# Another order of the seven block products of a feed-forward unit, and four extra buffers where its input sums are made

## The chip, the core and the metric

The kernel runs on one core of a Trainium2 chip. The metric is the device time of one execution in microseconds (us). The engines named below are PE (TensorE: matmuls, in its own order), ACT (ScalarE), DVE (VectorE), POOL (GpSimd) and SP, which issues the DMAs. Each takes its instructions in the order in which the program gives them to it.

## What is computed

The reference is a two-layer trunk over 512 latent and 256 context tokens of width 1024. Each layer has a gated feed-forward half (D_FF 2816), a mixer (a convolution in layer 0, neighbourhood attention in layer 1) and a second feed-forward half. The part that matters here:

```python
def _rmsnorm(x, g): return (x * rsqrt(mean(x * x) + 1e-6)) * g
def _ffn_half(s, mod, g, wg, wu, wd):
    shift, scale, gate = mod
    h = _rmsnorm(s, g) * (1 + scale) + shift
    return s + 0.5 * gate * ((silu(h @ wg) * (h @ wu)) @ wd)
def layer(i):
    x, xc = ffn_half(x, ...), ffn_half(xc, ...)      # first half
    x, xc = x + gate * mixer(x), xc + gate * mixer(xc)
    x, xc = ffn_half(x, ...), ffn_half(xc, ...)      # second half
```

Four feed-forward halves follow each other with the mixers between them. The change concerns the two in the middle (called ffn1 and ffn2 below: the second half of layer 0 and the first of layer 1), which run back to back.

## The kernel before

Activations lie with the 1024 channels on partitions (8 tiles `x0` to `x7` of 512 latent columns, 8 tiles `xc0` to `xc7` of 256 context columns). A matmul is made of three in a reduced fp32 format: an operand v is split into `hi` (a rounded copy, written by ACT) and `lo` (v minus hi, written by DVE), and hi*hi, hi*lo and lo*hi are added up in PSUM. `split` (L114 to L116) writes both parts.

In ffn1 and ffn2 the matrix product is done by a Strassen-like scheme with seven block products in place of eight. Channels and tokens are halved: columns are two blocks of 386 (384 tokens and two columns of shift). `s_prepare` (L445) makes, for each pair j of channel tiles (j = 0 to 3), the scaled activations `sx` and their sums and differences `tt`, and splits all of it: product 1 takes one block ("ones"), products 2 and 3 share a pair of tiles, so do 5 and 6, and 7 and 4. These tiles are slots of two rings: `h` (16 slots in pool main, which also hold `z`, the input of the product `pw2` at the end of the convolution, L806 to L828) and `hx` (12 slots). `s_prepare` runs in that loop after every second `pw2` product, and again in the last `down` loop of ffn1, for ffn2.

`s_weights` (L375) loads one weight unit, makes four sums in `s12` and `s34` on DVE (L398 to L402), and splits into four tiles, which this text calls A (products 1 and 2, from `raw`), B (6 and 5, from `s12`), C (7 and 3, from `s34`) and D (4, from `raw`, half as wide). `whi` and `wlo` are rings of three buffers, so A of the next unit takes the buffers of B, B those of C, C those of D, and D those of its own unit's A: each can be written once PE has finished the products of the tile before it in the buffer.

`s_unit` (L407) runs the seven products, 12 matmuls of 386 columns each, in three PSUM banks: x (`a`) holds 1, then 6 on top, 7 on top, 4 on top; y (`b`) holds 2; z (`c`) holds 5, then 3 on top. Between them partial sums leave the banks: `kept` (ACT, L422) copies one aside before the next product is added, and DVE adds rows (L429, L435, L437). A unit of the gate matrix (then a multiplication by `rb` on DVE, L487, and Silu on ACT, L489) and a unit of the up matrix make a pair; `s_ffn` (L475) runs groups of 2, 2, 2, 2 and 3 pairs, each followed by its `down` products (L125 to L127, L510). That is 11 pairs or 22 units in each of ffn1 and ffn2.

The order on each engine is not written by hand. The program is built with a scheduler that simulates the engines and emits whatever is ready by its own clock, so a changed order of the source moves instructions on all of them.

Of the kernel before, what the change touches and what calls it, by code (L numbers as in the profile page):

```python
# [23 lines left out]
T = TL + TC  # L24
# [3 lines left out]
BLK = 384  # L28
# [30 lines left out]
def tile_trunk(ctx: ExitStack, tc, xin, cb, cs, par, modp, modv, gu, gs, dn, pw1, pw2, wqk, wv, wo, bv, rpb, out):  # L59
# [38 lines left out]
    def X(c, s):  # L98
        return xc[c] if s else xl[c]
# [264 lines left out]
    def blocks(ap):  # L364
        return ap.rearrange("p (b n) -> p b n", b=2)
# [10 lines left out]
    def s_weights(src, pool):  # L376

        raws = []
        for i in range(2):
            raw = main.tile([P, 1024], F32, tag="raw", name="raw", bufs=4)  # L380
            nc.sync.dma_start(raw, src[i])
            raws.append(raw)
        q = [raws[0][:, :512], raws[0][:, 512:], raws[1][:, 512:], raws[1][:, :512]]
        s12 = pool.tile([P, 1024], F32, tag="s12", name="s12", bufs=1)
        s34 = pool.tile([P, 1024], F32, tag="s34", name="s34", bufs=1)
        s1, s2, s3, s4 = s12[:, 512:], s12[:, :512], s34[:, :512], s34[:, 512:]
        made = {}

        def parts_of(t, names):
            n = 512 * len(names)  # L390
            hi = main.tile([P, 1024], F32R, tag="whi", name="whi", bufs=3)
            lo = main.tile([P, 1024], F32R, tag="wlo", name="wlo", bufs=3)
            split(hi[:, :n], lo[:, :n], t[:, :n])
            for i, name in enumerate(names):
                made[name] = (hi, lo, 512 * i)

        parts_of(raws[0], (1, 2))
        nc.vector.tensor_tensor(s1, q[2], q[3], ALU.add)  # L398
        nc.vector.tensor_tensor(s2, s1, q[0], ALU.subtract)
        parts_of(s12, (6, 5))  # L400
        nc.vector.tensor_tensor(s3, q[0], q[2], ALU.subtract)
        nc.vector.tensor_tensor(s4, q[1], s2, ALU.subtract)  # L402
        parts_of(s34, (7, 3))
        parts_of(raws[1], (4,))
        return made

    def s_unit(src, hs, pool, row):  # L407

        made = s_weights(src, pool)

        def product(name, p, first):
# [24 lines left out]
        product(3, z, False)
        nc.vector.tensor_tensor(row[:, 0, 1], z, b, ALU.add)  # L437
        product(4, x, False)
        nc.scalar.activation(row[:, 1, 0], x, AF.Copy)

    def s_row(pool, tag):
        return pool.tile([P, 2, 2, SB], F32, tag=tag, name=tag, bufs=1)

    def s_prepare(j, hs, pool, A, B):

        sx = s_row(pool, "sg")
        tt = s_row(pool, "tu").rearrange("p a b n -> p (a b) n")
        for r in range(2):
            c = 2 * j + r
            for s in range(2):  # L450
                o, e, _ = PARTS2[s]
                nc.scalar.activation(sx[:, r, :, o:e], blocks(X(c, s)), AF.Identity, scale=A[:, s, c:c + 1])
            nc.gpsimd.tensor_copy(sx[:, r, :, BLK:], B[:, :, c].rearrange("p (a b) -> p a b", a=1).broadcast_to([P, 2, 2]))
        of = pool if j < 2 else None
        if j % 2 == 0:
            hs[1] = hs.get(1, []) + [None, None]
            ones_ = [slot() for _ in range(2)]
            for i in range(2):
                hs[1][j + i] = tuple(t[:, i * SB:(i + 1) * SB] for t in ones_)
        split(*hs[1][j], sx[:, 0, 0])  # L460

        def two(names, src):
            to = [slot(of) for _ in range(2)]
            split(*(t.rearrange("p (a n) -> p a n", a=2) for t in to), src)
            for i, n in enumerate(names):
                hs.setdefault(n, []).append(tuple(t[:, i * SB:(i + 1) * SB] for t in to))

        two((2, 3), sx[:, 1])
        nc.vector.tensor_tensor(tt[:, 0], sx[:, 0, 1], sx[:, 0, 0], ALU.subtract)
        nc.vector.tensor_tensor(tt[:, 1], sx[:, 1, 1], tt[:, 0], ALU.subtract)  # L470
        two((5, 6), tt[:, :2])
        nc.vector.tensor_tensor(tt[:, 2], sx[:, 1, 1], sx[:, 0, 1], ALU.subtract)
        nc.vector.tensor_tensor(tt[:, 3], sx[:, 1, 0], tt[:, 1], ALU.subtract)
        two((7, 4), tt[:, 2:])

    def s_ffn(idx, hs, hid, gate, done=None, tail=None):
        pair = 0
        for gi, gn in enumerate(PAIRS):
            last = gi == len(PAIRS) - 1
            hids = []  # L480
            f0 = 2 * pair
            for i in range(gn):
                sg, tu = s_row(hid, "sg"), s_row(hid, "tu")
                s_unit(gs[idx - 1, pair, 0], hs, hid, sg)
                for r in range(2):
                    so = sg[:, r, :, :BLK]
                    nc.vector.tensor_tensor(so, so, rbk, ALU.mult)  # L487
                    for o, e, s in PARTS2:
                        nc.scalar.activation(so[:, :, o:e], so[:, :, o:e], AF.Silu, bias=sg[:, r, 0, BLK + s:BLK + s + 1])  # L489
                s_unit(gs[idx - 1, pair, 1], hs, hid, tu)  # L490
                for r in range(2):
                    to = tu[:, r, :, :BLK]
                    if i < 2:
                        h2 = [hid.tile([P, T], F32R, tag="hid", name="hid", bufs=8) for _ in range(2)]
                    else:
                        h2 = [slot(hid if tail else None)[:, :T] for _ in range(2)]
                    h2 = [blocks(t) for t in h2]
                    nc.vector.tensor_tensor(to, to, rbk, ALU.mult)
                    for o, e, s in PARTS2:
                        nc.vector.scalar_tensor_tensor(to[:, :, o:e], to[:, :, o:e], tu[:, r, 0, BLK + s:BLK + s + 1],  # L500
                                                       sg[:, r, :, o:e], ALU.add, ALU.mult)
                    split(*h2, to)
                    hids.append(h2)
                pair += 1

            def down_one(d, w, st):
                o, e, s = PARTS2[st is CTX]
                p = pc(TC) if s else ps()
                mm3(blocks(p), w, [tuple(t[:, :, o:e] for t in h2) for h2 in hids], None, None)
                nc.vector.scalar_tensor_tensor(XS(d, st), p, derv[gate][:, s, d:d + 1], XS(d, st), ALU.mult, ALU.add)  # L510
                if last:
                    square_in(d, st)

            for sts in ((LAT,), (CTX,)) if last and tail else (BOTH,):
                for d in range(NC):
                    w = load(dn[idx, d, :, f0 * P:(f0 + 2 * gn) * P], 2 * gn * P)
                    for st in sts:
                        down_one(d, w, st)
# [286 lines left out]
    with tc.tile_pool(name="ffn12", bufs=1) as hid:  # L805
        hs = {}  # L806
        for d in range(NC):
# [16 lines left out]
            for st in BOTH:  # L824
                square_in(d, st)
            if d % 2:
                s_prepare(d // 2, hs, hid, derv[0, 7], mods[0, 6])
        s_rows(BOTH)  # L828

        hs2 = {}  # L830
# [301 lines left out]
```

## Time and profile before

| what | value |
|---|---|
| median of 3 runs | 2699.73 us (2698.58 to 2699.76) |
| the profiled execution, its own time | 2700.21 us |
| its span (first to last instruction in the trace) | 2698.4 us |
| PE busy | 2629.3 us, 97% of the span |
| DVE busy | 1905.2 us, 71% |
| ACT busy | 985.1 us, 37% |
| ffn1 and ffn2 with the end of the convolution | about 830 to 1990 us of the span |

A busy share says how long instructions of an engine were under way, not that it could not have been faster. What a wait costs is read from the idle time ahead of an instruction, in square brackets behind it in a timeline, with what ended it.

### The profile page before, as it was taken

The numbers are of one execution on the slowest core, as the hardware profiler recorded it, in microseconds if no ns is written. First come the engines' busy times: TensorE is split into PE (matmuls) and PEld (weight loads), VectorE is DVE, ScalarE is ACT, GpSimd is POOL, SyncE is SP. The second block draws the span as 40 slices with busy tenths as digits, with TensorE's granted clock in tenths as the row PEclk, the third lists the DMA queues.
The fourth block names the chain that finished last, engine by engine and source line by source line (L and its number), as shares of the span: only waits on it lengthen the run. The fifth ranks groups of instructions, "written<-read, shape, count | busy, mean of one in ns | idle before, by whom it ended". The sixth has DMA issues, their size and how long they took to land.

```text
span 2698.4 us, 40901 instructions
## 1 busy us (share of the span) xinstructions
PE 2629.3 (97%) x16420; PEld 2358.1 (87%) x16420; DVE 1905.2 (71%) x3268; ACT 985.1 (37%) x1601; POOL 77.5 (3%) x140
## 2 busy tenths in 40 slices
PE   8999999999989899999999999999999999999997
PEld 4888888888859799999999999999888888999997
DVE  4999999857996766666777666667677576544446
ACT  4212121232226533433454234334446365322224
POOL 0000000011020100000001000000000000000001
PEclk9999999999999899999999999999999999999999
DMA  8565656622351122122121221221332211233223
GB/s 303 167 205 171 207 174 229 235 73 84 97 119 48 36 75 67 55 78 67 61 80 40 82 67 51 71 80 59 116 101 62 64 61 48 72 103 100 87 96 108
DMA packets 97262, 276.66 MB, mean 103 GB/s; under 512 B 11568, under 2 KB 26032, under 8 KB 96944
## 3 DMA queue, kind: packets, MB, share of 16 engines
q1 hardware_dynamic: 96496, 272.48, 31.7%
q8 instruction: 129, 2.11, 0.3%
q0 software_dynamic: 576, 1.57, 0.2%
q14 instruction: 61, 0.50, 0.1%
HBM read 268.05 MB, written 4.38 MB: 101 GB/s over the span
## 4 chain that ended last, share of the span: by engine, by line
PE 90%; DVE 4%; issue 2%; ACT 2%; DMA 1%; POOL 1%; SPq 0%; DVEq 0%; POOLq 0%; ACTq 0%
PE a L417 13%; PE a L125 8%; PE a L127 8%; PE a L126 8%; PE c L417 6%; PE c L125 6%; PE c L126 6%; PE c L127 6%; PE b L125 5%; PE b L126 5%; PE b L127 5%; PE b L417 3%; PE st L975 2%; PE b L966 1%; DVE y L691 1%
## 5 line engine op out<-in xcount | busy, mean ns | idle before, releaser
L110 ACT ACTIVATE whi<-raw 128x1024 fp32r<-128x1024 f32 (+3 forms) x304 | 270.0, 891 | 862.2 <-PE c L126 454.3
L111 DVE TENSOR_TENSOR wlo<-raw,whi 128x1024 fp32r<-128x1024 f32 (+3 forms) x304 | 306.0, 1009 | 89.8 <-ACT whi L110 87.7
L549 DVE SCALAR_TENSOR_TENSOR junk<-mraw,sbc 128x1024 f32<-128x1024 f32 x224 | 272.8, 1218 | 1.7
L125 PE MATMUL a<-h,whi 128*128 128x512 f32 (+2 forms) x826 | 270.0, 328 | 1.1 <-DVE sg L301 1.1
L127 PE MATMUL a<-h,wlo 128*128 128x512 f32 (+2 forms) x826 | 269.0, 326 | 0.9 <-DVE wlo L111 0.9
L126 PE MATMUL a<-h,whi 128*128 128x512 f32 (+2 forms) x826 | 269.0, 326 | 0.0
L417 PE MATMUL a<-h,whi 128*128 128x386 f32 x880 | 234.8, 345 | 21.9 <-ACT whi L115 19.5
L125 PE MATMUL c<-h,whi 128*128 128x258 f32 (+2 forms) x768 | 233.1, 306 | 1.2 <-ACT h L115 1.1
L126 PE MATMUL c<-h,whi 128*128 128x258 f32 (+2 forms) x768 | 233.3, 305 | 0.6 <-DVE h L116 0.6
L127 PE MATMUL c<-h,wlo 128*128 128x258 f32 (+2 forms) x768 | 232.4, 303 | 0.0
L417 PEld LDWEIGHTS a<-h,whi 128*128 128x128 f32 x880 | 160.0, 190 | 30.9 <-ACT whi L115 26.2
L125 PE MATMUL b<-h,whi 128*128 128x512 f32 (+2 forms) x550 | 181.7, 330 | 5.3 <-ACT h L237 3.4
L126 PE MATMUL b<-h,whi 128*128 128x512 f32 (+2 forms) x550 | 180.8, 329 | 0.5 <-DVE h L238 0.5
L127 PE MATMUL b<-h,wlo 128*128 128x512 f32 (+2 forms) x550 | 180.4, 328 | 0.0
L115 ACT ACTIVATE whi<-s 128x1024 fp32r<-128x1024 f32 x88 | 93.5, 1062 | 229.1 <-PE c L417 126.7
L125 PEld LDWEIGHTS a<-h,whi 128*128 128x128 f32 x826 | 155.8, 189 | 16.9 <-DVE sg L301 2.0
L127 PEld LDWEIGHTS a<-h,wlo 128*128 128x128 f32 x826 | 156.1, 189 | 15.6 <-DVE wlo L111 1.6
L126 PEld LDWEIGHTS a<-h,whi 128*128 128x128 f32 x826 | 156.2, 189 | 14.1 <-issue 0.8
L126 PEld LDWEIGHTS c<-h,whi 128*128 128x128 f32 x768 | 145.3, 189 | 8.6 <-DVE h L116 1.2
L125 PEld LDWEIGHTS c<-h,whi 128*128 128x128 f32 x768 | 144.1, 188 | 9.6 <-ACT h L115 1.5
L127 PEld LDWEIGHTS c<-h,wlo 128*128 128x128 f32 x768 | 145.7, 190 | 6.6 <-issue 0.6
L417 PE MATMUL a<-h,wlo 128*128 128x386 f32 x440 | 149.4, 340 | 0.0
(305 smaller groups left out, 6388.7 us busy)
## 6 DMA issues: line engine op xcount, KB each, us to landing
mraw<-in_modv SPq DMA_DIRECT2D x128, 512.0 KB
raw<-in_gu SPq DMA_DIRECT2D x88, 512.0 KB
raw<-in_gs SPq DMA_DIRECT2D x88, 512.0 KB
raw<-in_dn SPq DMA_DIRECT2D x64, 384.0 KB
raw<-in_dn SPq DMA_DIRECT2D x64, 256.0 KB
raw<-in_pw SPq DMA_DIRECT2D x24, 512.0 KB
raw<-in_dn SPq DMA_DIRECT2D x32, 320.0 KB
us<-v SPq DMA_DIRECT2D x64, 142.0 KB
```

The source lines that it names most:

```text
L110: nc.scalar.activation(hi[:, :cols], raw[:, :cols], AF.Copy)
L111: nc.vector.tensor_tensor(lo[:, :cols], raw[:, :cols], hi[:, :cols].bitcast(F32), ALU.subtract)
L115: nc.scalar.activation(hi, src, AF.Copy)
L125: nc.tensor.matmul(po, lhsT=whi[:, s], rhs=ah, start=first and i == 0, stop=False)
L126: nc.tensor.matmul(po, lhsT=whi[:, s], rhs=al, start=False, stop=False)
L127: nc.tensor.matmul(po, lhsT=wlo[:, s], rhs=ah, start=False, stop=last and i == k - 1)
L417: nc.tensor.matmul(p, lhsT=a[:, k], rhs=b, start=first and j == 0 and i == 0, stop=j == 3 and i == 2, skip_group_check=True)
L549: nc.vector.scalar_tensor_tensor(junk, raw, 1.0, sbc[:, s, :], ALU.mult, ALU.mult, accum_out=m[:, s, c:c + 1])
L691: nc.vector.scalar_tensor_tensor(yo, u[:, k:k + n], w, yo, ALU.mult, ALU.add)
L966: nc.tensor.transpose(pt[:, i * P:(i + 1) * P], p[:, i * P:(i + 1) * P], ident)
L975: nc.tensor.matmul(po[64 * a:64 * a + 64, :P], lhsT=v[:, c0:c0 + 64], rhs=PT[a][:, i * P:(i + 1) * P], start=i == 0, stop=i == 3)
```

## The change

In `s_unit` the order of the products is 1, 2, 5, 6, 3, 7, 4 in place of 1, 2, 6, 5, 7, 3, 4. In `s_prepare` the call at the end of the convolution (`early=True`) takes `sx` and `tt` from the ring `hid` (8 buffers, so two j are under way at once; `hid` tiles become 772 wide in place of 768) and no longer from the single `sg` and `tu`. The slots are dealt out otherwise: "ones" of all j, (2, 3) of j 0 and 1, and (5, 6) and (7, 4) of j 0 come from `hx`, all others from `h`; before, all of j 0 and 1 but "ones" came from `hx`, and "ones" and all of j 2 and 3 from `h`. In `s_weights` two DVE subtractions change places.

```diff
@@ s_weights
+        nc.vector.tensor_tensor(s4, q[1], s2, ALU.subtract)
         nc.vector.tensor_tensor(s3, q[0], q[2], ALU.subtract)
-        nc.vector.tensor_tensor(s4, q[1], s2, ALU.subtract)
@@ s_unit
+        product(5, z, True)
+        d = kept(z)
         product(6, x, False)
         b = kept(x)
-        product(5, z, True)
-        d = kept(z)
+        product(3, z, False)
+        nc.vector.tensor_tensor(row[:, 0, 1], z, b, ALU.add)
         product(7, x, False)
         nc.vector.tensor_tensor(row[:, 1, 1], x, d, ALU.add)
-        product(3, z, False)
-        nc.vector.tensor_tensor(row[:, 0, 1], z, b, ALU.add)
         product(4, x, False)
@@ s_prepare
-    def s_prepare(j, hs, pool, A, B):
-        sx = s_row(pool, "sg")
-        tt = s_row(pool, "tu").rearrange("p a b n -> p (a b) n")
+    def s_prepare(j, hs, pool, A, B, early=False):
+        if early:
+            sx = [pool.tile([P, TB], F32, tag="hid", name="sx", bufs=8) for _ in range(2)]
+            tt = [pool.tile([P, TB], F32, tag="hid", name="tt", bufs=8) for _ in range(2)]
...
-        of = pool if j < 2 else None
-            ones_ = [slot() for _ in range(2)]
+            ones_ = [slot(pool) for _ in range(2)]
...
-        two((2, 3), sx[:, 1])
+        two((2, 3), sx[1], pool if j < 2 else None)
...
-        two((5, 6), tt[:, :2])
+        two((5, 6), tt[0], pool if j < 1 else None)
...
-        two((7, 4), tt[:, 2:])
+        two((7, 4), tt[1], pool if j < 1 else None)
@@ end of the convolution
-                s_prepare(d // 2, hs, hid, derv[0, 7], mods[0, 6])
+                s_prepare(d // 2, hs, hid, derv[0, 7], mods[0, 6], True)
```

First place: PE in the second group of ffn1, where a gate unit passes into its up unit. Before (bank `a_9394` is x of the gate unit, `c_9396` its z, `a_9523` and `b_9524` are x and y of the up unit, `whi_9503` is the up unit's A, `whi_9386` the gate unit's C):

```order
L417 MATMUL a_9394<-h_8518,whi_9380 128x386
L417 MATMUL a_9394<-h_8519,whi_9380 128x386
L417 MATMUL a_9394<-h_8518,wlo_9381 128x386
L417 MATMUL c_9396<-h_8518,wlo_9381 128x386
L417 MATMUL a_9523<-h_7840,whi_9503 128x386
L417 MATMUL a_9523<-h_7841,whi_9503 128x386
L417 MATMUL b_9524<-hx_7844,whi_9503 128x386
L417 MATMUL b_9524<-hx_7845,whi_9503 128x386
L417 MATMUL a_9394<-hx_7856,whi_9386 128x386
```

The same place in the changed program (`a_9402` and `c_9404` are x and z of the gate unit, `whi_9394` its C, `whi_9511` the up unit's A):

```order
L417 MATMUL a_9402<-h_8526,whi_9388 128x386
L417 MATMUL a_9402<-h_8527,whi_9388 128x386
L417 MATMUL a_9402<-h_8526,wlo_9389 128x386
L417 MATMUL c_9404<-hx_7846,whi_9394 128x386
...
L417 MATMUL c_9404<-h_8520,wlo_9395 128x386
L417 MATMUL a_9531<-hx_7842,whi_9511 128x386
L417 MATMUL a_9531<-hx_7843,whi_9511 128x386
L417 MATMUL b_9532<-hx_7846,whi_9511 128x386
L417 MATMUL b_9532<-hx_7847,whi_9511 128x386
L417 MATMUL a_9402<-hx_7858,whi_9394 128x386
```

The first four matmuls of the up unit, which need its A, stood right behind products 6 and 5; now the 12 matmuls of product 3 stand between.

Second place: ACT and DVE where the up unit of that pair passes into the gate unit of the next. ACT before, from the up unit's C (`whi_9515`) to the next gate unit's A (`whi_9642`); L439 and L489 still belong to the gate unit of the first pair:

```order
L115 ACTIVATE whi_9515<-s34_9502 128x1024
L439 ACTIVATE sg_9366<-a_9394 128x386
L115 ACTIVATE whi_9519<-raw_9499 128x512
L489 ACTIVATE sg_9366<-sg_9366 128x2x256
L489 ACTIVATE sg_9366<-sg_9366 128x2x128
L422 ACTIVATE kept_9565<-a_9523 128x386
L115 ACTIVATE whi_9642<-raw_9636 128x1024
```

ACT in the changed program (Silu is L494 there), from the up unit's C (`whi_9523`) to the next gate unit's A (`whi_9650`):

```order
L115 ACTIVATE whi_9523<-s34_9510 128x1024
L115 ACTIVATE whi_9527<-raw_9507 128x512
L439 ACTIVATE sg_9374<-a_9402 128x386
L422 ACTIVATE kept_9573<-c_9533 128x386
L494 ACTIVATE sg_9374<-sg_9374 128x2x256
L494 ACTIVATE sg_9374<-sg_9374 128x2x128
L115 ACTIVATE whi_9650<-raw_9644 128x1024
```

The two Silu instructions now stand right ahead of the next unit's A. DVE at the same place, before (L487 is the multiplication that the Silu waits for):

```order
L116 TENSOR_TENSOR wlo_9516<-s34_9502,whi_9515 128x1024
L487 TENSOR_TENSOR sg_9366<-sg_9366,rb_81 128x2x384
L429 TENSOR_TENSOR tu_9367<-b_9524,kept_9538 128x386
L116 TENSOR_TENSOR wlo_9520<-raw_9499,whi_9519 128x512
L401 TENSOR_TENSOR s34_9641<-raw_9636,raw_9638 128x512
L402 TENSOR_TENSOR s34_9641<-raw_9636,s12_9640 128x512
```

and in the changed program (that multiplication is L492 there):

```order
L116 TENSOR_TENSOR wlo_9524<-s34_9510,whi_9523 128x1024
L401 TENSOR_TENSOR s34_9649<-raw_9644,s12_9648 128x512
L402 TENSOR_TENSOR s34_9649<-raw_9644,raw_9646 128x512
L116 TENSOR_TENSOR wlo_9528<-raw_9507,whi_9527 128x512
L492 TENSOR_TENSOR sg_9374<-sg_9374,rb_81 128x2x384
```

Two sums and the lo part of D moved ahead of the multiplication.

Third place: PE right behind the last `pw2` product. Before, the first unit began with matmuls on tiles of several j and products mixed:

```order
L417 MATMUL b_8587<-hx_7844,whi_8566 128x386
L417 MATMUL b_8587<-hx_7845,whi_8566 128x386
L417 MATMUL b_8587<-hx_7844,wlo_8567 128x386
L417 MATMUL c_8588<-hx_7850,whi_8572 128x386
L417 MATMUL c_8588<-hx_7851,whi_8572 128x386
L417 MATMUL a_8586<-h_7840,whi_8566 128x386
```

In the changed program product 1 of all four j comes first, from `hx` alone (the rows show the last two j, `hx_8292` and `hx_8293`, and the start of product 2):

```order
L417 MATMUL a_8594<-hx_8292,whi_8574 128x386
L417 MATMUL a_8594<-hx_8293,whi_8574 128x386
L417 MATMUL a_8594<-hx_8292,wlo_8575 128x386
L417 MATMUL b_8595<-hx_7846,whi_8574 128x386
L417 MATMUL b_8595<-hx_7847,whi_8574 128x386
```

Up to the `pw2` loop, and from the last `down` loop of ffn2 on, all engines have the same instructions in the same order as before.

## Rows read from the trace of the kernel before

**Rows 1.** The page: the span, and busy time of each engine.
```profile
span 2698.4 us, 40901 instructions
PE 2629.3 (97%) x16420; PEld 2358.1 (87%) x16420; DVE 1905.2 (71%) x3268; ACT 985.1 (37%) x1601; POOL 77.5 (3%) x140
```

**Rows 2.** Windows: stretch, length, busy time (instructions) by engine, PE clock, DMA.
```profile
880.00:890.00 10.00, 7.03 (x37) 5.79 (x36) 8.63 (x14) 8.72 (x16) 2.00 (x2) 0.85 0.00 0
890.00:900.00 10.00, 7.63 (x15) 3.70 (x14) 8.02 (x15) 7.03 (x13) 6.19 (x17) 0.50 0.00 1
...
1600.00:1700.00 100.00, 98.19 (x560) 92.66 (x559) 65.30 (x93) 34.54 (x53) 0.00 (x0) 1.00 0.24 75
```

**Rows 3.** Waits of PE in 900:1400 and in 1450:1900: total, times, longest.
```profile
PE a L417 <- ACT whi L115: 10.2, 11, 1.0
...
PE a L417 <- ACT whi L115: 9.2, 10, 1.0
```

**Rows 4.** Timeline of PE in ffn1: start, duration, instruction, idle time before.
```profile
913.17 0.52 PE L417 MATMUL a<-hx,whi 128*128 128x386 f32 x2
...
915.28 0.51 PE L417 MATMUL b<-hx,whi 128*128 128x386 f32 x2
...
937.16 0.63 PE L417 MATMUL a<-h,whi 128*128 128x386 f32 x2 [1.02 <-ACT whi L115]
```

**Rows 5.** Timeline of ACT in ffn1.
```profile
915.37 1.06 ACT L115 ACTIVATE whi<-s 128x1024 fp32r<-128x1024 f32 x1 [0.67 <-PE a L417]
...
918.59 1.13 ACT L489 ACTIVATE sg<-sg 128x512 f32<-128x512 f32 x2 [1.01 <-DVE sg L487]
919.62 0.47 ACT L422 ACTIVATE kept<-a 128x386 f32<-128x386 f32 x1
...
936.05 1.06 ACT L115 ACTIVATE whi<-raw 128x1024 fp32r<-128x1024 f32 x1 [3.31 <-issue]
```

**Rows 6.** Timeline of DVE in ffn1.
```profile
909.40 0.56 DVE L435 TENSOR_TENSOR sg<-a,kept 128x386 f32<-128x386 f32 x1 [2.00 <-PE a L417]
...
916.46 1.22 DVE L116 TENSOR_TENSOR wlo<-s,whi 128x1024 fp32r<-128x1024 f32 x1 [0.88 <-ACT whi L115]
917.61 0.95 DVE L487 TENSOR_TENSOR sg<-sg,rb 128x768 f32<-128x768 f32 x1
...
919.54 0.68 DVE L401 TENSOR_TENSOR s<-raw 128x512 f32<-128x512 f32 x1
920.15 0.68 DVE L402 TENSOR_TENSOR s<-raw,s 128x512 f32<-128x512 f32 x1
```

**Rows 7.** Timeline of PE from the end of pw2 to the first unit's product 6.
```profile
880.72 0.51 PE L417 MATMUL b<-hx,whi 128*128 128x386 f32 x2
...
884.23 0.45 PE L417 MATMUL a<-h,whi 128*128 128x386 f32 x1 [1.75 <-ACT h L115]
...
897.36 2.04 PE L206 MATMUL st<-t,ones 128*128 128x512 f32 x2 [1.83 <-DVE t L200]
...
904.89 0.34 PE L417 MATMUL a<-h,wlo 128*128 128x386 f32 x1
```

**Rows 8.** Timelines of ACT, DVE and POOL in that stretch.
```profile
878.56 0.52 ACT L115 ACTIVATE h<-sg 128x386 fp32r<-128x386 f32 x1
...
888.31 1.83 DVE L116 TENSOR_TENSOR hx<-tu,hx 128x772 fp32r<-128x772 f32 x2
...
896.25 0.96 DVE L200 TENSOR_TENSOR t<-ident,nwt 128x768 f32<-128x768 f32 x1 [1.79 <-POOL nwt L189]
...
879.80 0.31 POOL L453 COPY sg<-mod 128x4 f32<-128x4 f32 x2 [47.21 <-DVE h L116]
888.12 2.19 POOL L453 COPY sg<-mod 128x4 f32<-128x4 f32 x2 [8.00 <-DVE hx L116]
890.40 0.49 POOL L180 TENSOR_SCALAR nwt<-nwt 128x6 int32<-128x6 int32 x1
```

**Rows 9.** Timeline of PE where ffn1 passes into ffn2.
```profile
1437.94 1.10 PE L206 MATMUL st<-t,ones 128*128 128x512 f32 x2 [1.30 <-DVE t L200]
```

More of the change, by code (lines that the diff above doesn't have):

```diff
@@ L442, in s_row @@
         return pool.tile([P, 2, 2, SB], F32, tag=tag, name=tag, bufs=1)
-    def s_prepare(j, hs, pool, A, B):
-        sx = s_row(pool, "sg")
-        tt = s_row(pool, "tu").rearrange("p a b n -> p (a b) n")
+    def s_prepare(j, hs, pool, A, B, early=False):
+        if early:
+            sx = [pool.tile([P, TB], F32, tag="hid", name="sx", bufs=8) for _ in range(2)]
+            tt = [pool.tile([P, TB], F32, tag="hid", name="tt", bufs=8) for _ in range(2)]
+            sx, tt = ([t.rearrange("p (b n) -> p b n", b=2) for t in ts] for ts in (sx, tt))
+        else:
+            sx, tt = s_row(pool, "sg"), s_row(pool, "tu")
+            sx, tt = ([t[:, r] for r in range(2)] for t in (sx, tt))
         for r in range(2):
@@ L451, in s_prepare, with two @@
                 o, e, _ = PARTS2[s]
-                nc.scalar.activation(sx[:, r, :, o:e], blocks(X(c, s)), AF.Identity, scale=A[:, s, c:c + 1])
-            nc.gpsimd.tensor_copy(sx[:, r, :, BLK:], B[:, :, c].rearrange("p (a b) -> p a b", a=1).broadcast_to([P, 2, 2]))
-        of = pool if j < 2 else None
+                nc.scalar.activation(sx[r][:, :, o:e], blocks(X(c, s)), AF.Identity, scale=A[:, s, c:c + 1])
+            nc.gpsimd.tensor_copy(sx[r][:, :, BLK:], B[:, :, c].rearrange("p (a b) -> p a b", a=1).broadcast_to([P, 2, 2]))
         if j % 2 == 0:
             hs[1] = hs.get(1, []) + [None, None]
-            ones_ = [slot() for _ in range(2)]
+            ones_ = [slot(pool) for _ in range(2)]
             for i in range(2):
                 hs[1][j + i] = tuple(t[:, i * SB:(i + 1) * SB] for t in ones_)
-        split(*hs[1][j], sx[:, 0, 0])
-        def two(names, src):
+        split(*hs[1][j], sx[0][:, 0])
+        def two(names, src, of=None):
             to = [slot(of) for _ in range(2)]
@@ L466, in two @@
                 hs.setdefault(n, []).append(tuple(t[:, i * SB:(i + 1) * SB] for t in to))
-        two((2, 3), sx[:, 1])
-        nc.vector.tensor_tensor(tt[:, 0], sx[:, 0, 1], sx[:, 0, 0], ALU.subtract)
-        nc.vector.tensor_tensor(tt[:, 1], sx[:, 1, 1], tt[:, 0], ALU.subtract)
-        two((5, 6), tt[:, :2])
-        nc.vector.tensor_tensor(tt[:, 2], sx[:, 1, 1], sx[:, 0, 1], ALU.subtract)
-        nc.vector.tensor_tensor(tt[:, 3], sx[:, 1, 0], tt[:, 1], ALU.subtract)
-        two((7, 4), tt[:, 2:])
+        two((2, 3), sx[1], pool if j < 2 else None)
+        nc.vector.tensor_tensor(tt[0][:, 0], sx[0][:, 1], sx[0][:, 0], ALU.subtract)
+        nc.vector.tensor_tensor(tt[0][:, 1], sx[1][:, 1], tt[0][:, 0], ALU.subtract)
+        two((5, 6), tt[0], pool if j < 1 else None)
+        nc.vector.tensor_tensor(tt[1][:, 0], sx[1][:, 1], sx[0][:, 1], ALU.subtract)
+        nc.vector.tensor_tensor(tt[1][:, 1], sx[1][:, 0], tt[0][:, 1], ALU.subtract)
+        two((7, 4), tt[1], pool if j < 1 else None)
     def s_ffn(idx, hs, hid, gate, done=None, tail=None):
@@ L493, in s_ffn @@
                     if i < 2:
-                        h2 = [hid.tile([P, T], F32R, tag="hid", name="hid", bufs=8) for _ in range(2)]
+                        h2 = [hid.tile([P, TB], F32R, tag="hid", name="hid", bufs=8)[:, :T] for _ in range(2)]
                     else:
```

## The prediction

> **What bounds the kernel now.** I read the page first: PE is busy for 2629.3 of 2698.4 us [rows 1], so whatever is not PE's own work shows as a hole in PE. The change removes no matmul, so it can only fill holes. Windows of 100 us say where they are: in the steady part of ffn1 and ffn2 PE is busy for 98.19 of 100 us, at full clock; at the end of the convolution two windows of 10 us hold only 7.03 and 7.63 us of PE work, and the second runs at a granted clock of 0.50, half of 2.4 GHz [rows 2]. These are the two places that the change touches.
>
> The list of waits names the steady hole: PE waits for ACT's `whi` (L115) 21 times, 19.4 us together [rows 3]. The timeline shows the mechanism. One matmul of 386 columns takes 0.176 us (12 in the 2.11 us from 913.17 to 915.28), and a wait of 1.02 us stands ahead of the matmul at 937.16 [rows 4]. It is released by the ACT split at 936.05 [rows 5], tile A of the next unit. By the order shown, that is the up unit's product 1 placed right behind products 6 and 5 of the gate unit. But A goes into the buffer of B, so the split can only begin when 6 and 5 have ended, and the matmul starts 937.16 - 936.05 = 1.11 us later. This happens once in a pair, in 21 of 22 pairs.
>
> At the end of the convolution PE finishes `pw2` at 880.72 and product 6 of the first unit at 904.89 + 0.18 = 905.07 [rows 7]. Between them lie 48 matmuls (1, 2, 5 and 6), 48 x 0.176 = 8.4 us of work at full clock, in 24.3 us. It waits for splits of the activations: those in `h` can't begin before `pw2` lets go of `z`, and the first, at 878.56, comes only then [rows 8].
>
> **What the change does, and what each part costs.**
>
> 1. *The gate unit's wait goes.* Product 3 now lies between product 6 and the next A: 12 x 0.176 = 2.11 us of cover against 1.11 us of need. ACT has one `kept` copy behind A and nothing slow ahead of it. I take away all 19.4 us. Bounds: nothing, if ACT comes more than 1.0 us late; all of it.
>
> 2. *A new wait at the up unit.* Before, A of the next gate unit was needed behind product 7 of the up unit; now behind its product 3. What must come first is counted from the end of the gate unit's product 4, which frees C's buffer. ACT's C begins 0.09 us later (915.28 to 915.37), DVE's lo part 1.09 after that (916.46), and holds DVE for 1.15 (to 917.61) [rows 4 to 6]. Then by the new order come two sums and the lo part of D, 0.61 each (919.54 to 920.15 [rows 6]; D's is as wide), 1.83; the multiplication, 0.98 until Silu starts (917.61 to 918.59); the Silu pair, 1.03 (918.59 to 919.62 [rows 5]); and A, 1.11 until the matmul. Sum: 0.09 + 1.09 + 1.15 + 1.83 + 0.98 + 1.03 + 1.11 = 7.28 us. PE's cover from product 4's end are products 5, 6 and 3 of the up unit, 36 matmuls or 6.34 us (34 where the scheduler put two of product 5 ahead of product 4). That leaves a wait of 0.94 us. It needs a gate unit that follows an up unit in its group: 1 in each group of two pairs and 2 in the group of three, 6 for each of ffn1 and ffn2. 12 x 0.94 = 11.3 us come back. Behind the last pair of a group come `down` weights of half the width (no sums, shorter split), which the same count puts ahead of need. Bounds: 0, if ACT gets to A ahead of the Silu; 12 x 1.5 = 18, if DVE is 0.6 us (one more instruction of that width) later.
>
> 3. *Product 4 right behind 7 on the same bank.* It must wait for DVE to read x (L435 and L437). DVE begins that read 0.27 us after product 7 (909.13 by pitch, 909.40 [rows 6]) and takes 0.56. The order puts 20 matmuls of the next unit between (3.5 us), or 12 of `down` in the last unit of a group. Cost nothing; without that cover it would be 0.9 us in each of 44 units.
>
> 4. *End of the convolution.* Everything of j 0, (2, 3) and "ones" of j 1 and half of j 2 can now be split under `pw2`, which has room: nothing there waits for `z`. Left for DVE after its first `h` tile (878.56 + 0.84 of ACT = 879.4) and ahead of the last operand of product 6 are 7 splits of 772 columns at 0.92 (888.31, 1.83 for two [rows 8]), C's lo 1.15, four differences of 386 columns at about 0.5, two sums at 0.61, and three additions for x7, xc7 and the rms sums, about 1.4 by their width: 6.4 + 1.15 + 2.0 + 1.2 + 1.4 = 12.2, so until 891.6; a few tenths of waiting for ACT and four matmuls bring product 6 to its end at about 892.6. Against 905.07 that is 12.5 us gained. What was hidden there before now lies on the path: the rms sums are spread by L206, which stood in PE's waiting time and now comes inside product 7. POOL's reciprocal square root takes 890.40 to 896.25 and PE follows 1.11 us later [rows 7, 8]; started some 0.8 us later than before it holds PE back by about 0.8 us, and L206 itself costs 1.0 (2.04 at half clock). The first up unit has one multiplication more in the count of part 2, and two matmuls less of cover: 1.2 us. For a stretch at half clock I allow 1.0. So 12.5 - 0.8 - 1.0 - 1.2 - 1.0 = 8.5 us gained. Bounds: nothing, if DVE's work was the limit all along; 11.5 if neither clock nor L206 costs anything and PE waits 2 us less.
>
> 5. *ffn1 into ffn2.* `s_prepare` isn't early there. But L206 now stands ahead of the end of product 6 and not behind product 7, so 16 fewer matmuls (2.8 us) cover POOL, where PE already waits 1.30 us [rows 9]; DVE's start of that chain stands about four instructions (2.3 us) earlier. 2.8 - 2.3, and a little clock: 1.0 us lost, between 0 and 3.
>
> 6. The swap of two subtractions, the wider `hid` tiles and the new slots change no duration; both subtractions end before C is split.
>
> Sum: 19.4 - 11.3 + 8.5 - 1.0 = 15.6 us. The profiled execution took 2700.21, so 2684.6; the median of the runs is 0.5 lower, so **2684.0 us**.
>
> **A rule to weigh.** DVE and POOL disturb each other here: two bias copies of 4 columns took 0.31 us with DVE idle and 2.19 with DVE busy, and the first step of the root 0.49 [rows 8]. The Trainium skill, "SBUF — State Buffer", section "Who interferes with whom", has the rule: a DVE instruction with two SBUF inputs and a GpSimd instruction that reads SBUF exclude each other, and the loser is blocked for the whole instruction. That agrees with the copies, and it speaks against the change, which packs DVE fuller just where POOL runs. By the rule alone all 13 steps of the root would wait for a DVE split of 0.92 each, 12 us in place of 5.85, and the sum would be about 2690, an estimate by that page; by the rows only part of them do, and the sum is 2684.0.
>
> **The rivals.**
> - *The second wait doesn't come*: ACT reaches A in time. For it: the sum of part 2 exceeds the cover by 0.94 of 7.28 us only. Against it: ACT takes the Silu first by the order shown. Time 2684.0 - 11.3 - 1.2 = 2671.5.
> - *DVE gains nothing by starting early*: the queue after `pw2` is as long as before. For it: DVE is busy 8.63 and 8.02 of 10 us there already [rows 2]. Against it: half of its splits have left. Time 2684.0 + 8.5 = 2692.5.
> - *POOL is held up*: about five steps of the root fall beside full DVE; each waits for one split of 0.92: 4.6 us on PE at L206. For it the 2.19 us copies, against it that DVE's queue thins out behind product 6. Time 2688.6.
> - *Slower*: DVE's read of x comes late and product 4 waits, in the 34 units where 20 matmuls cover it. It decides from 3.5 us after product 7 on; at 4.0 us every unit loses 0.5, 17 us in all, which eats the whole gain: 2701, and slower beyond. Against it: DVE now begins 0.27 us behind product 7, and is 65% busy [rows 2].
> - *The change doesn't do what it says*: the waits move without a net gain (part 2 at its upper bound, part 4 near nothing, ffn2 losing 3): 19.4 - 18 - 3 + 2 = 0.4 us, 2699.
>
> **How the numbers follow.** Less than 0.2% (5.4 us) is what a measurement of this kernel can't tell from no change. The forecast, with its own spread of 2678 to 2689, gets 0.52; no second wait 0.14; POOL held up 0.12; nothing from the early start 0.11; no net change 0.07; slower 0.04. The first four are faster by more than 0.2% (2694.3 or less): 0.89; same 0.07; slower 0.04. The range goes from the second case to the edge of the fourth: 2671 to 2694.
>
> **What would show it.** In the changed profile the waits of PE for ACT L115 in ffn1 and ffn2 should be about 12, near 0.9 us each, ahead of a gate unit's product 1 and behind product 3, with Silu (L494) right ahead of that split; none at the up unit. The first unit's product 6 should end near 892.6, 12 us after `pw2`, and PE should wait for L200 behind it. If there are no such waits, part 2 is wrong; if there are many longer ones, DVE's place in that chain is worse than counted; if product 6 ends near 900, part 4 is. The stages ahead of `pw2` and behind ffn2 should be as they were; a difference there would mean that the change reaches further than its instructions do.

## The result, and the profile after

The changed kernel takes 2664.84 us (median of 4 runs, 2664.33 to 2665.06) against 2699.3 us for the kernel before beside it (2698.58 to 2699.76): a ratio of 0.9872, 95% interval 0.9855 to 0.9889. The gain of 34.5 us is more than twice the forecast of 15.6, and the time lies below the lower end of the range (2671).

The page of the changed kernel, its span and its engines' busy time, beside [rows 1]:

```profile
span 2663.3 us, 40955 instructions
PE 2616.7 (98%) x16420; PEld 2357.5 (89%) x16420; DVE 1918.7 (72%) x3268; ACT 988.3 (37%) x1601; POOL 87.9 (3%) x140
```

The same windows as [rows 2] (columns as there):

```profile
880.00:890.00 10.00, 8.72 (x52) 8.06 (x50) 9.49 (x16) 7.18 (x12) 0.60 (x1) 1.00 0.00 0
890.00:900.00 10.00, 9.76 (x43) 8.83 (x44) 6.04 (x9) 4.00 (x7) 4.87 (x13) 0.83 0.33 105
...
1600.00:1700.00 100.00, 100.00 (x570) 95.73 (x570) 67.31 (x93) 37.92 (x57) 0.00 (x0) 1.00 0.23 71
```

Busy time of PE falls by 12.6 us only, but the steady window went from 98.19 to 100.00 of 100 us and holds 570 matmuls in place of 560: no hole is left there. At the end of the convolution PE is busy for 8.72 and 9.76 of 10 us, and the second window runs at a granted clock of 0.83, where it ran at 0.50. The five largest waits of PE from 860 to 1960, the end of the convolution and both feed-forwards (total, times, longest), beside [rows 3]:

```profile
PE a L417 <- ACT hx L115: 2.1, 1, 2.1
PE b L911 <- ACT h L264: 1.5, 1, 1.5
PE c L417 <- DVE h L116: 0.8, 1, 0.8
PE b L417 <- DVE h L116: 0.7, 1, 0.7
PE a L417 <- ACT kept L422: 0.6, 1, 0.6
```

The split into `whi` at L115, waited for 21 times and 19.4 us before, isn't in the list of this stretch at all: the old wait is gone, and the twelve new ones of the forecast aren't there.

Where the time came from is read by laying the two timelines of PE side by side. Both kernels have the same matmuls, so the n-th of one answers to the n-th of the other wherever the order is the same. Before: a matmul in `pw2` (number 5,601 on PE), the first matmul of groups 2 and 3 of ffn1, of ffn2, of group 2 of ffn2, and one in ffn2's last `down` (number 11,401):

```profile
871.53 0.29 PE L125 MATMUL c<-h,whi 128*128 128x256 f32 x1
...
992.00 0.52 PE L417 MATMUL a<-h,whi 128*128 128x386 f32 x2
...
1087.27 0.52 PE L417 MATMUL a<-h,whi 128*128 128x386 f32 x2
...
1420.93 0.52 PE L417 MATMUL a<-h,whi 128*128 128x386 f32 x2
...
1522.80 0.52 PE L417 MATMUL a<-h,whi 128*128 128x386 f32 x2
...
1938.22 0.28 PE L127 MATMUL c<-hid,wlo 128*128 128x256 f32 x1
```

The same six after:

```profile
869.91 0.29 PE L125 MATMUL c<-h,whi 128*128 128x256 f32 x1
...
978.40 0.51 PE L417 MATMUL a<-hx,whi 128*128 128x386 f32 x2
...
1071.25 0.51 PE L417 MATMUL a<-hx,whi 128*128 128x386 f32 x2
...
1396.21 0.52 PE L417 MATMUL a<-hx,whi 128*128 128x386 f32 x2
...
1499.35 0.51 PE L417 MATMUL a<-hx,whi 128*128 128x386 f32 x2
...
1903.98 0.28 PE L127 MATMUL c<-hid,wlo 128*128 128x256 f32 x1
```

The lead grows from 1.62 to 13.60, to 24.72, falls to 23.45 and ends at 34.24 us. So four stages can be told apart (S1 from the first of these matmuls to the second, S2 from the second to the fourth, S3 to the fifth, S4 to the sixth):

| stage | before | after | gain | waits gone |
|---|---|---|---|---|
| S1: end of the convolution, group 1 of ffn1 | 120.47 | 108.49 | 11.98 | 2 |
| S2: the rest of ffn1 | 428.93 | 417.81 | 11.12 | 9 |
| S3: group 1 of ffn2 | 101.87 | 103.14 | -1.27 | 1 |
| S4: the rest of ffn2 to its last `down` | 415.42 | 404.63 | 10.79 | 9 |

A group of two pairs takes 1087.27 - 992.00 = 95.27 us before and 1071.25 - 978.40 = 92.85 after: 2.42 us for its two waits, 1.21 for one. At that price 21 waits are 25.4 us, the end of the convolution gained 11.98 - 2.42 = 9.6, and the passage into ffn2 lost 1.27 + 1.21 = 2.5. Together 32.5 us. What the two profiles differ by beyond that lies ahead of the first of the six rows (1.62 us) and behind the last (0.9), where the matmuls did not change. Ahead of the first the profile of before happened to run late: the kernel with the order alone, below, has the program of before up to `pw2` and reached that matmul at 869.52. Behind the last, the kernels below take between 759.1 and 760.5 us, so 0.9 us there says nothing.

### The profile page after: what moved, and what is told of

Its sections match the earlier page's. It is cut to its first block, busy times and chain, and to the rows that moved or that the text cites. A ratio compares the mean times of both kernels' runs of the same rounds, so it can differ in the third digit from the quotient of the medians.

```text
span 2663.3 us, 40955 instructions
## 1 busy us (share of the span) xinstructions
PE 2616.7 (98%) x16420; PEld 2357.5 (89%) x16420; DVE 1918.7 (72%) x3268; ACT 988.3 (37%) x1601; POOL 87.9 (3%) x140
## 3 DMA queue, kind: packets, MB, share of 16 engines
q8 instruction: 129, 2.11, 0.3%
## 4 chain that ended last, share of the span: by engine, by line
PE 93%; DVE 4%; ACT 1%; issue 1%; DMA 1%; POOL 0%; SPq 0%; DVEq 0%; POOLq 0%; ACTq 0%
PE a L417 14%; PE a L125 8%; PE a L127 8%; PE a L126 8%; PE c L417 7%; PE c L125 6%; PE c L126 6%; PE c L127 6%; PE b L125 5%; PE b L126 5%; PE b L127 5%; PE b L417 3%; PE st L980 2%; DVE y L696 1%; PE b L971 1%; PE c L714 1%
## 5 line engine op out<-in xcount | busy, mean ns | idle before, releaser
L110 ACT ACTIVATE whi<-raw 128x1024 fp32r<-128x1024 f32 (+3 forms) x304 | 270.1, 891 | 869.3 <-PE c L126 446.8
L417 PE MATMUL a<-h,whi 128*128 128x386 f32 x792 | 205.0, 339 | 0.0
L125 PEld LDWEIGHTS a<-h,whi 128*128 128x128 f32 x826 | 155.8, 189 | 16.9 <-DVE sg L301 2.0
L126 PEld LDWEIGHTS a<-h,whi 128*128 128x128 f32 x826 | 156.1, 189 | 14.0 <-issue 0.8
L417 PE MATMUL a<-hx,whi 128*128 128x386 f32 x616 | 162.8, 340 | 2.7 <-ACT hx L115 2.1
L115 ACT ACTIVATE whi<-s 128x1024 fp32r<-128x1024 f32 x88 | 93.5, 1062 | 172.9 <-PE a L417 79.1
L417 PEld LDWEIGHTS a<-h,whi 128*128 128x128 f32 x792 | 144.9, 189 | 0.0
```

Of the source, the lines that this page charges most:

```text
L110: nc.scalar.activation(hi[:, :cols], raw[:, :cols], AF.Copy)
L115: nc.scalar.activation(hi, src, AF.Copy)
L125: nc.tensor.matmul(po, lhsT=whi[:, s], rhs=ah, start=first and i == 0, stop=False)
L126: nc.tensor.matmul(po, lhsT=whi[:, s], rhs=al, start=False, stop=False)
```

## The experiments

Stages of every run, worked out as above from its own timeline; the times are medians, the ratios are against the kernel before beside it (2698.8 to 2699.2 us).

| kernel | us | ratio (95%) | S1 | S2 | S3 | S4 |
|---|---|---|---|---|---|---|
| order_only | 2675.33 | 0.9912 (0.9897 to 0.9927) | 117.85 | 417.43 | 103.77 | 404.77 |
| early_only | 2692.66 | 0.9973 (0.9963 to 0.9983) | 109.90 | 428.69 | 105.86 | 415.23 |
| temps_only | 2665.61 | 0.9876 (0.9862 to 0.9891) | 107.12 | 417.66 | 103.02 | 405.33 |
| slots_only | 2672.70 | 0.9901 (0.9885 to 0.9918) | 114.03 | 418.52 | 103.64 | 405.58 |
| noswap | 2665.67 | 0.9878 (0.9861 to 0.9894) | 108.51 | 417.81 | 103.25 | 404.63 |
| rotate | 2676.04 | 0.9914 (0.9899 to 0.9929) | 108.08 | 417.83 | 102.88 | 404.67 |
| rotate_cd | 2675.47 | 0.9909 (0.9893 to 0.9926) | 108.84 | 417.83 | 103.58 | 404.64 |
| dose0f | 2666.19 | 0.9878 (0.9864 to 0.9893) | 108.55 | 418.09 | 103.11 | 404.63 |
| dose2f | 2671.20 | 0.9897 (0.9882 to 0.9912) | 109.67 | 419.38 | 103.95 | 406.08 |
| bias_act | 2668.17 | 0.9887 (0.9873 to 0.9902) | 109.30 | 417.80 | 106.67 | 404.59 |
| bias_dve | 2667.01 | 0.9881 (0.9866 to 0.9895) | 108.53 | 417.81 | 104.67 | 404.63 |
| mix | 2665.85 | 0.9876 (0.9862 to 0.9891) | 109.39 | 417.80 | 103.53 | 404.59 |
| mix_temps | 2665.91 | 0.9876 (0.9860 to 0.9893) | 107.12 | 417.66 | 103.01 | 405.32 |

### One part alone: order_only and early_only

order_only is the kernel before with the new `s_unit` and `s_weights` of the diff and the old `s_prepare`; early_only is the other half.

> The kernel before with the new order of the products and the swapped subtractions, the end of the convolution left as it was. Ledger theory (the parts pay separately, and a wait costs about 0.26 us more than its idle row): all 21 waits for the split of A go, 21 x 1.2 = 25.2 us, the passage from the first to the second feed-forward loses 2.5, the end of the convolution stays: about 2676.6 us, no wait of PE for L115 in the steady part. Rival (the second wait is only hidden because the early buffers change the timing): about 12 waits near 0.9 us come back at the gate units, 2690. Rival (the new order also costs at the end of the convolution, as it does between the two feed-forwards): 2679.

> The changed kernel with the old order of the products and of the two subtractions; only the early buffers and slots at the end of the convolution stay. Ledger theory: the 21 waits of about 0.9 us for the split of A are back; the end of the convolution keeps its gain of 9 to 10 us, and the passage between the feed-forwards is as before: about 2689.8 us, product 6 of the first unit ends near 893. Rival (the gain at the end of the convolution needs the new order too, since product 5 stands ahead of product 6 there): 2693 or more.

The order alone is worth 23.8 us, as the ledger had it (22.7 forecast): S2 and S4 are those of the changed kernel, no wait for `whi` of L115 is left, so the second wait stays away without the early buffers too. S1 gains 2.62, which is its two waits and next to nothing else: the end of the convolution stays as it was, its stretch at half clock too. The window of order_only from 890 to 900:

```profile
890.00:900.00 10.00, 7.82 (x17) 4.58 (x17) 8.09 (x13) 6.99 (x12) 4.50 (x12) 0.50 0.00 0
```

That of early_only:

```profile
890.00:900.00 10.00, 8.92 (x36) 7.70 (x37) 6.10 (x10) 3.98 (x6) 5.50 (x13) 0.83 0.32 105
```

With the order alone that stretch runs at a clock of 0.50, as before, and at 0.83 with the early buffers. early_only gains 10.6 us in S1 and holds its waits in S2 and S4, so that far the ledger is right; but its time is 2692.7 and not 2689.8. Its wait for the split of A, from 900 to 1960:

```profile
PE a L417 <- ACT whi L115: 18.5, 20, 1.0
```

and that for the spread of the rms sums, from 1400 to 1440:

```profile
PE st L206 <- DVE t L200: 3.2, 1, 3.2
```

That wait at the passage was 1.30 before [rows 9], and S3 is 4.0 us longer than before. By time the parts make 23.8 + 6.5 = 30.3 of the 34.3 us; by stages they gain 1.2 us more than the whole change in S1 and lose 4.6 us more in S3, so what they miss lies at the passage. The time is near the rival's 2693, but not for its reason, since S1 keeps its gain without the new order. Six of the eight runs lie at 2692.6 to 2693.1, the other two at 2688.5 and 2689.3, near the forecast; which of its waits makes the step stays open.

### The two halves of the early part, and the swap: temps_only, slots_only, noswap

```diff
-            ones_ = [slot(pool) for _ in range(2)]
+            ones_ = [slot() for _ in range(2)]
...
-        two((5, 6), tt[0], pool if j < 1 else None)
+        two((5, 6), tt[0], pool if j < 2 else None)
...
-        two((7, 4), tt[1], pool if j < 1 else None)
+        two((7, 4), tt[1], pool if j < 2 else None)
```

is temps_only against the changed kernel; slots_only calls `s_prepare` without `True`, and noswap puts the two subtractions back.

> The changed kernel with its four extra buffers and its order of products, but with the slots of the sums as before (the ones of j 0 and 1 in the slots that wait for z; (5,6) and (7,4) of j 1 in the early ones). Theory (the room for the sums of two j at once is what gains at the end of the convolution): about as the changed kernel, one split of 772 columns later, 2666 us. Rival (the slots are what gains, since the ones of j 0 hold back the rest): near the kernel with the order alone, 2672 to 2675 us.

> The changed kernel with its new slots and its order of products, but with the sums in the two single tiles of before, so that the sums of one j must be split before those of the next are made. Theory (the buffers gain): j 2 and j 3 stay in series behind pw2, about 2672 us, product 6 of the first unit ends 8 us or more later than in the changed kernel. Rival (the slots gain): 2666 us.

> The changed kernel with the two subtractions of the weight sums in their old order. Both stand ahead of the split of C, which reads both. Theory: no difference, 2665 us within 1. Rival (the difference that product 7 needs first comes later by 0.6 us and PE waits for C): 2665 + up to 44 x 0.1 = 2669.

The buffers gain nearly all: 2665.61 with the buffers alone, 2672.70 with the slots alone, 2675.33 with neither. The slots are worth 2.6 us by themselves and nothing that can be told beside the buffers. The window from 890 to 900 of temps_only:

```profile
890.00:900.00 10.00, 9.36 (x47) 8.28 (x48) 7.35 (x11) 4.34 (x7) 4.84 (x13) 1.00 0.29 105
```

and of slots_only:

```profile
890.00:900.00 10.00, 9.16 (x27) 7.20 (x28) 7.10 (x11) 5.29 (x9) 3.36 (x10) 0.62 0.13 48
```

Both are busy for some 9 of 10 us, but in one PE gets through 47 matmuls and in the other through 27, since the clock is 1.00 and 0.62: a busy PE says little where the clock fell. temps_only is 1.4 us better than the changed kernel in S1 and gives 0.7 back in S4, where its matmuls stand in the same order; the time is equal within what can be told. The swap does nothing (2665.67).

### Does the second wait come if C has to wait for product 4? rotate and rotate_cd

In rotate the three buffers of `whi` and of `wlo` are handed out in strict turn; rotate_cd adds the last line.

```diff
+    def wnext(): wturn[0] += 1; return wturn[0] % 3
...
-        hi = main.tile([P, 1024], F32R, tag="whi", name="whi", bufs=3)
+        hi = main.tile([P, 1024], F32R, tag=f"whi{wnext()}", name="whi", bufs=1)
...
+            if names == (4,): nc.scalar.activation(hi[:, :1], made[7][0][:, :1].bitcast(F32), AF.Copy)
```

> The changed kernel with the weight buffers handed out in strict rotation, so that tile C of an up unit must wait for product 4 of the unit before, and with one tiny copy that keeps tile D behind C on ACT. Theory (the second wait stayed away only because C took the buffer that product 2 had freed, 2.1 us earlier): PE waits again for the split of A at the gate units that follow an up unit, 12 times near 0.9 us by the idle row, about 1.2 us each in time: 2665 + 14 = 2679 us. Rival (the chain of splits, multiplication and Silu has room to spare anyway): no such waits, 2665 us.

> The changed kernel with the weight buffers handed out in strict rotation and nothing else, so that the scheduler is free to put D ahead of C on ACT: the partner of the run before. Theory: with D's lo part and the sums out of the way of the multiplication the chain from product 4 is about 1.8 us shorter than 7.28 us and fits into the 6.34 us of cover: no waits, 2665 us within 2. Rival (any C that waits for product 4 is late): 2679 us.

The time of rotate_cd looks like my theory (2675.5, forecast 2679), but the place is wrong: S2 to S4 are those of the changed kernel within 0.5 us, and PE waits for no `whi` of L115 from 900 on. rotate, which was to cost nothing, lost as much. The 11 us were lost ahead of the feed-forward (the first product of ffn1 starts at 889.82 in rotate_cd, in place of 879.10). There the strict turn holds up other weights: from 500 to 880 PE waits 8.4 us for `whi` of L110, and 0.8 in the changed kernel. So my theory fell: the second wait stays away although C now waits. ACT in rotate_cd at one up unit; product 4 of the unit before ends at 1008.50:

```profile
1008.58 1.06 ACT L115 ACTIVATE whi<-s 128x1024 fp32r<-128x1024 f32 x1 [3.27 <-PE a L417]
...
1011.80 1.13 ACT L494 ACTIVATE sg<-sg 128x512 f32<-128x512 f32 x2 [0.31 <-DVE sg L492]
1012.84 1.04 ACT L115 ACTIVATE whi<-raw 128x1024 fp32r<-128x1024 f32 x1
```

DVE there:

```profile
1009.67 1.22 DVE L116 TENSOR_TENSOR wlo<-s,whi 128x1024 fp32r<-128x1024 f32 x1 [1.84 <-ACT whi L115]
1010.82 0.95 DVE L492 TENSOR_TENSOR sg<-sg,rb 128x768 f32<-128x768 f32 x1
1011.68 0.68 DVE L116 TENSOR_TENSOR wlo<-raw,whi 128x512 fp32r<-128x512 f32 x1
```

C begins behind product 4, but the multiplication (L492) now stands right behind C's lo part and ahead of D's lo part and the two sums. The chain is 1.83 us shorter, and A is split at 1012.84 for a matmul at 1014.86. The scheduler had put DVE's queue in another order to fit.

### Lengthening the chain: dose0f and dose2f

dose0f adds two one-column copies on ACT that hold A behind the Silu; dose2f adds two multiplications by one on DVE ahead of that Silu.

```diff
+            if dep and names == (1, 2): nc.scalar.activation(hi[:, :1], dep[0], AF.Copy)
...
+                nc.scalar.activation(deps[0], sg[:, 1, 0, :1], AF.Copy)
...
+                    [nc.vector.tensor_scalar(so, so, 1.0, None, ALU.mult) for _ in range(2 * r)]
```

> The changed kernel with two copies of one column on ACT (about 0.2 us each) that force the split of A of a gate unit to come behind the Silu of the unit before, which is where it stands already. In the changed kernel A's matmul could start 0.92 us before it is needed. Theory (that slack is real): no wait, 2665 us within 1.5. Rival (the chain is at its limit): 12 waits of some 0.3 us, 2669 us. It is the partner of the next run.

> As the run before, with two further multiplications by one of 768 columns on DVE (about 0.95 us each by the row of the multiplication there) between the multiplication and the Silu of the second half, so that the chain that leads to A is 1.9 us longer; they do not change the values. Theory (chain of 7.28 us that starts at product 2, so with 0.92 us of slack, 0.5 behind the two copies): A comes 1.4 us late 12 times, 12 x 1.5 = 18 us, about 2683 us, and PE waits about 1.2 us each time ahead of product 1 of a gate unit. Rival (the wait never comes, since the chain has room for more): 2665 to 2667 us.

dose0f is as expected, 2666.2. dose2f costs 5.0 us more and not 17: the two multiplications took 1.16 us together and not 1.9, and no gate unit waits for its A: from 900 on PE waits for a weight split of L115 or L116 only twice, 0.3 us each, at the passage into ffn2. Its split of A at one gate unit:

```profile
1006.24 1.06 ACT L115 ACTIVATE whi<-raw 128x1024 fp32r<-128x1024 f32 x1
```

and PE at that place (L416 is the matmul of the products in this kernel):

```profile
1006.30 0.51 PE L416 MATMUL a<-hx,whi 128*128 128x386 f32 x2
...
1008.41 0.51 PE L416 MATMUL a<-hx,whi 128*128 128x386 f32 x2
```

The matmul at 1006.30 is the first of product 7, and that at 1008.41 the first of the next unit's product 1: all of product 7 now lies ahead of it, 2.11 us of cover, where the changed kernel has the next unit's first four matmuls (two of product 1, two of product 2) ahead of product 7. A matmul that needs this A could start 1.11 us behind the split, at 1007.35, so in the old place, at 1006.30, it would have waited. What it costs, 4.7 us over S1 to S4 beside dose0f, is spread over the groups. So here too the scheduler gave way, on PE this time, and there is no run in which the wait of the forecast comes.

### The passage into ffn2: bias_act, bias_dve, mix, mix_temps

The passage lost more than forecast. bias_act and bias_dve move the copies of L458 off POOL; mix and mix_temps take the old order of products in ffn2's first unit alone, with the slots of the changed kernel and of temps_only.

```diff
-            nc.gpsimd.tensor_copy(sx[r][:, :, BLK:], B[:, :, c].rearrange("p (a b) -> p a b", a=1).broadcast_to([P, 2, 2]))
+            nc.scalar.activation(sx[r][:, :, BLK:], B[:, :, c].rearrange("p (a b) -> p a b", a=1).broadcast_to([P, 2, 2]), AF.Copy)
```

```diff
-                s_unit(gs[idx - 1, pair, 0], hs, hid, sg)
+                s_unit(gs[idx - 1, pair, 0], hs, hid, sg, idx == 2 and pair == 0)
...
+        for n in (6, 5, 7, 3) if old else (5, 6, 3, 7):
```

> The changed kernel with the bias copies of 4 columns (L458) on ACT instead of POOL. In the changed kernel's trace one pair of them took 4.53 us on POOL beside a full DVE at the passage between the two feed-forwards, and PE then waited 2.1 us for the splits behind them and ran a stretch at half clock. Theory (these copies are what the passage waits for): that wait goes, and some of the half-clock stretch with it, 3 us or more: about 2661.5 us. Rival (DVE's queue of splits sets the passage): within 1 us of the changed kernel, 2664 to 2665.

> The same with the bias copies on DVE, where they add 16 short instructions of some 0.16 us to the queue of splits. Theory (POOL's wait for DVE is what costs): nearly the gain of the run before, about 2662 us. Rival (DVE's queue sets the passage): 2665 us or a little more.

> The changed kernel with the old order of the products in one unit alone, the first of the second feed-forward. In the changed kernel's trace that unit takes 20.8 us from its product 1 to the next unit's, where it took 17.6 before, and PE holds full clock again only at its end. Theory (the passage loses 2 to 3 us because products 6 and 3 now stand where 7 did, ahead of the splits' end): those come back, about 2662.5 us. Rival (the loss is in the queue of splits on DVE and in the root on POOL, which the order does not touch): 2664 to 2666.

> As the run before, with the slots of the kernel before at the end of the convolution (which alone made 2665.6). Theory: the two do not touch each other, so again 2 to 3 us below 2665.6, about 2663. Rival (the order does not set the passage): 2665 to 2666.

None gains. bias_act makes S3 3.5 us longer, and its waits from 1390 to 1430 show where the old one went:

```profile
PE st L206 <- DVE t L200: 3.1, 1, 3.1
PE a L417 <- DVE hx L116: 1.4, 1, 1.4
```

The wait of 2.1 us for ACT's `hx` has become one of 1.4 for DVE's part of it, and behind it PE waits 3.1 us for L200, the spread of the rms sums, which it did not in the changed kernel. The old order in that unit moves S3 by 0.4 us or less. So the passage gets no shorter by taking the copies off POOL, which puts them on ACT or DVE, nor by the order of that unit. S3 lies between 102.9 and 104.0 in every kernel with the new order but the two with moved copies. What the 2.5 us hang on stays open. No version was faster than the changed kernel.

## Why the prediction was wrong

**Step 1, mis-sized.** The waits went, all 21, but they were worth 25.4 us and not 19.4. I took the idle time that the row prints for the price. Two rows of before around the wait of 1.02 us at 937.16 [rows 4] show what it leaves out:

```profile
935.81 0.34 PE L417 MATMUL a<-h,wlo 128*128 128x386 f32 x1
...
937.63 0.52 PE L417 MATMUL b<-hx,whi 128*128 128x386 f32 x2
```

Matmuls follow each other every 0.176 us, but a row lasts 0.34, and idle time is counted from its end: the hole is 937.16 - 935.81 - 0.176 = 1.17 us. The two matmuls behind it then take 937.63 - 937.16 = 0.47 in place of 0.35. Together 1.29 for a printed 1.02, and 21 x 0.27 is 5.7 of the 6.0 us.

**Step 2, the step that failed.** The forecast put back 11.3 us for twelve new waits, and none came. Of my chain of 7.28 us the durations held (7.54 below) and the start did not. The up unit that begins at 988.98 in the changed kernel, first PE (product 4 of the unit before, then product 1 of the next):

```profile
995.33 0.52 PE L417 MATMUL a<-hx,whi 128*128 128x386 f32 x2
...
1003.79 0.51 PE L417 MATMUL a<-hx,whi 128*128 128x386 f32 x2
```

ACT, with C, D, the Silu and the next unit's A:

```profile
995.42 1.06 ACT L115 ACTIVATE whi<-s 128x1024 fp32r<-128x1024 f32 x1 [1.11 <-PE b L417]
997.45 0.63 ACT L115 ACTIVATE whi<-raw 128x512 fp32r<-128x512 f32 x1 [0.97 <-PE a L417]
...
1000.73 1.12 ACT L494 ACTIVATE sg<-sg 128x512 f32<-128x512 f32 x2 [0.25 <-DVE sg L492]
1001.76 1.05 ACT L115 ACTIVATE whi<-raw 128x1024 fp32r<-128x1024 f32 x1
```

DVE, from C's lo part to the multiplication:

```profile
996.68 1.22 DVE L116 TENSOR_TENSOR wlo<-s,whi 128x1024 fp32r<-128x1024 f32 x1
997.93 0.69 DVE L401 TENSOR_TENSOR s<-raw,s 128x512 f32<-128x512 f32 x1
...
999.14 0.69 DVE L116 TENSOR_TENSOR wlo<-raw,whi 128x512 fp32r<-128x512 f32 x1
999.75 0.95 DVE L492 TENSOR_TENSOR sg<-sg,rb 128x768 f32<-128x768 f32 x1
```

C is split at 995.42, released by bank b, which is product 2 of the same unit. Product 4 of the unit before only begins at 995.33, and its end releases D at 997.45. So, by these releasers, in the changed kernel the up unit's C takes the buffer of its own unit's A, and D that of the last D: I had read from the trace of before that C takes D's, but there product 4 came ahead of product 2, and by the new order it comes behind it. It is so at all twelve places, and in order_only too: product 2 releases C, and A stands right behind the Silu, as forecast, but in time. From 995.33 the links of the sum lead to 1001.76 for A and, with 1.11 behind it, to 1002.87, 0.92 us ahead of the matmul at 1003.79; from product 4's end at 997.43 they would have led to 1.2 us behind it (0.9 by the 7.28 of the forecast). Half of my sum came from one program's buffers and half from the other's order. rotate_cd says that this is not all: with C held to product 4, DVE's order is another one, and no wait comes either. That the order of the changed program would have been late with C behind product 4 is worked out, not shown.

**Step 3** was right: no row shows a wait of product 4, and S2 and S4 leave nothing for one.

**Step 4** was nearly right: 9.6 us against 8.5. Product 6 of the first unit ends at 891.5 and not 892.6; with the 1.62 us by which the profile of before ran late that is 893.1 on its scale, a gain of 11.9 of the 12.5 counted. Of that 2.3 us were lost again, where I had charged 4.0. PE there, after (the last matmul of product 6, and the spread of the rms sums):

```profile
891.21 0.53 PE L417 MATMUL a<-h,wlo 128*128 128x386 f32 x1
...
897.51 1.02 PE L206 MATMUL st<-t,ones 128*128 128x512 f32 x2
```

POOL there (a pair of bias copies, the first and the last step of the root):

```profile
842.05 9.76 POOL L458 COPY sx<-mod 128x4 f32<-128x4 f32 x2 [10.83 <-DVE tt L477]
...
889.40 0.84 POOL L180 TENSOR_SCALAR nwt<-nwt 128x6 int32<-128x6 int32 x1 [28.94 <-DVE nwt L178]
...
895.66 0.20 POOL L189 TENSOR_TENSOR nwt<-nwt 128x6 f32<-128x6 f32 x1
```

L206 has no idle time ahead of it: the wait for the root that I charged with 0.8 didn't come, and the 1.2 for the first up unit fell with step 2. The stretch at half clock did come (0.50 from 891 to 893). The root took 889.40 to 895.86, 6.5 us in place of 5.85: three of its 13 steps took 0.84, 1.58 and 1.05 us, the others 0.20. So of the rival "POOL is held up" a delay of 0.6 us came in place of 4.6, and PE did not wait for it. By the rule of the Trainium skill, "SBUF — State Buffer", section "Who interferes with whom", the root alone would have taken 12 us, as I estimated from it with every step blocked. The trace agrees with the rule for the three long steps: each began while DVE ran a split and ended within 0.1 us of the end of one (892.19, for the 1.58, and 892.12). The other ten began beside none.

**Step 5** was under-sized, 2.5 us lost for 1.0 forecast, within its bounds of 0 to 3. The reason I gave, L206 ahead of product 6's end, isn't what the trace shows: PE waits 2.1 us for the splits of `hx` and not for L200. **Step 6** was right (noswap).

The forecast's 15.6, with 6.0 from step 1, 11.3 from step 2, 1.1 from step 4 and -1.5 from step 5, makes 32.5; the other 2.0 of the 34.5 lie in the stretches whose matmuls did not change. The rival "the second wait doesn't come" had the event, with a chance of 0.14, but not its reason, the earlier buffer of C; its 2671.5 lacked the 6.0 us of step 1.

## What to carry to other kernels

Price a wait by the starts on both sides of it, less one pitch, with the slow matmul behind it, and not by the idle time of a row: here the two differ by 0.27 us in 1.29, 21 times over. Which buffer a tile gets is part of the order: where the order of two releases turns round, the tiles behind them change buffers, so a chain has to be read from one program from end to end. The scheduler that simulates the engines emitted another order where, by my sums, a changed program would have opened a wait, on DVE in one run here and on PE in another, so a new wait that is 13% of its chain deserves a smaller chance than an old one that stands in the trace.

## What was not expected of the hardware

Two copies of 4 columns on POOL took 9.76 us at 842.05, and 4.53 at the passage, beside a busy DVE, where four of them took 0.56 us with nothing in the way. The first pair ended at 851.81, in DVE's first pause since they began (851.63 to 851.99). Taking them off POOL gained nothing; that DVE's queue of splits sets the pace there is my reading, and no run shows it by itself. And PE at full busy share is not PE at full speed: 27 matmuls in 9.16 us of busy time at a granted clock of 0.62, against 47 in 9.36 at 1.00.
